# Four layer-norm joints of a two-layer decoder: a split accumulator, a sum read in place, and one centring moved to ScalarE and GpSimd

## The chip, the core and the metric

The kernel runs on one core of a Trainium2 chip. The metric is the device time of one execution in microseconds (us), lower is better. The program is a static list of instructions for each engine: TensorE (PE; its weight loads are listed as PEld), VectorE (DVE), ScalarE (ACT), GpSimd (POOL) and SyncE (SP), which issues most of the DMAs. Each engine works through its own list in order and waits on semaphores for the others.

## The reference

Two layers over 256 positions of 1024 features, all float32. Layer 0 mixes with latent attention, layer 1 with a three-branch sparse attention. Behind each mixer comes a PEER feed-forward block, and after every sub-layer a post-norm, so there are four layer norms:

```python
h = layer_norm(ALPHA * h + mix, ln_g[layer, 0], ln_b[layer, 0])
ffn = peer_ffn(h, p_w_q[layer], p_subkeys[layer], p_u[layer], p_v[layer])
h = layer_norm(ALPHA * h + ffn, ln_g[layer, 1], ln_b[layer, 1])

def layer_norm(x, g, b):
    mu = jnp.mean(xf, axis=-1, keepdims=True)
    var = jnp.mean(jnp.square(xf - mu), axis=-1, keepdims=True)
    return ((xf - mu) * lax.rsqrt(var + LN_EPS) * g + b)
```

The PEER block scores 16384 experts for each token by two sets of 128 sub-keys, keeps 16 for each of 8 heads, and returns the sum of the rows of `p_v` for these experts, weighted by gate times gelu of the dot product with the rows of `p_u`.

## The kernel before

The 256 tokens are two tiles of 128 (`tt` 0 and 1). The kernel computes a PEER block densely: a u phase of 128 steps forms the activations of all experts for most tokens (plain float32 matmuls of 160 columns), and a v phase of 128 steps (`j`) multiplies the gated activations with the rows of `p_v`. The last 64 tokens are done by gathered rows instead (GpSimd's indirect DMAs and VectorE's multiply-accumulate into `gacc`).

**The v phase.** Each step takes a block of `p_v` of 128 rows and 1024 columns. It is split into a high and a low half in the matmul's rounded float32 format (`hi` by ScalarE, line 179; `lo` by VectorE, line 193), and so are the activations (`W`). `v_mm` then issues the matmuls: for token tile 0 three products (high x high, high x low, low x high), for tile 1 two, each over two blocks of 512 columns. Tile 1 holds only 64 tokens that are computed densely; its stationary operand `W[:, P:2P]` carries their high part in one half of its columns and their low part in the other, so its accumulator has the high part's result in partitions 0 to 63 and the low part's in 64 to 127, and the two are added at the end. The accumulators `accs[tt][f]` are four PSUM banks (`pacc`), and four more banks (`mm`, handed out by `self.ps()` in turn) serve everything else.

The last ten steps keep their operands (`keep`), and do tile 0 only. Then tile 0's layer norm runs on VectorE while TensorE catches up with tile 1: the last three steps first, then for the column blocks `f` = 0 and 1 in turn the other seven.

**The joint.** I call the stretch around a layer norm a joint. There are four: two behind the mixers (`out_close`), one behind each PEER block. Behind a PEER block, `sum_1(f)` adds tile 1's block to the residual `hN`: ScalarE copies partitions 64 to 127 of the accumulator to a spare bank (line 988), VectorE adds ALPHA times the residual and the first half (989), then the copy (990), and `ln_stats` takes the statistics of 512 columns (347). `ln_mid` (all four joints) aggregates them (356), takes the square root on ScalarE (357), centres and multiplies the first half by the gain (351), and works out the reciprocal root in short steps of one column (360 to 363). `ln_scale` scales and shifts each half (369); for the second half it first centres (351 again). Where a layer follows (`want_T`), `ln_T` transposes each half on TensorE (line 300), ScalarE casts it into `hT` (383) and VectorE takes the low part (384), and `early_mm` starts the next block's matmuls in between. In the last joint the halves are stored instead (line 371). `lo_aside` has GpSimd do one subtraction of the next block's weights (line 193 on POOL) in the three joints that have a successor.

The order on every engine is that of the code; there is no scheduler.

## Time and profile before

| | |
|---|---|
| median of 3 runs | 1603.38 us (1600.02 to 1606.42) |
| profiled execution | 1603.88 us, span 1601.9 us |
| TensorE busy | 1557.4 us, 97% of the span, 10018 matmuls |
| VectorE busy | 1396.6 us, 87% |
| ScalarE, GpSimd busy | 683.6 us (43%), 536.3 us (33%) |
| matmuls of 512 columns on `hi` and `W` | 1452, line 273 |

A row of the timeline gives the start and the duration in us, the engine, the line of the kernel, the operation, the tile written and the tiles read, the shape, and a count where like instructions are merged; in brackets stands how long the engine had been idle and whom it waited for. Durations of matmuls are modelled and overlap; the distance between their starts is what they cost. A row of a view by windows gives for each engine the busy time and, in brackets, the number of instructions, then TensorE's granted clock (1.00 is full), the DMA engines' share and GB/s.

### The profile page before, as it was taken

How to read it: one execution, taken by the hardware profiler on the slowest of the kernel's cores; microseconds unless marked ns; L12 is line 12 of the kernel's file. 1: busy time of each engine (PE TensorE's matmuls, PEld its weight loads, DVE VectorE, ACT ScalarE, POOL GpSimd, SP SyncE). 2: the span in 40 equal slices, each digit the busy share in tenths (PEclk: the TensorE clock that was granted, in tenths of full speed). 3: DMA queues.
4: the chain of work that ended last, by engine and by line, in shares of the span. 5: the costliest groups of instructions: out<-in, count | busy, mean ns of one | idle time of the engine just before them, and what ended most of it. 6: DMA issues, size and time to landing. Idle time of an engine off the chain costs nothing.

```text
span 1601.9 us, 27548 instructions
## 1 busy us (share of the span) xinstructions
PE 1557.4 (97%) x10018; PEld 1396.3 (87%) x10018; DVE 1396.6 (87%) x3245; ACT 683.6 (43%) x1355; POOL 536.3 (33%) x442
## 2 busy tenths in 40 slices
PE   8999999999999999999997999999999999999997
PEld 6879999999998888888785689999999988888886
DVE  5778898999959999999768779799999959999998
ACT  6555201121225555556456753111221245555553
POOL 2010134434326434340442210234443337543420
PEclk9999999999999999999999999999999999999999
DMA  7627899999999999997573257999999999999992
GB/s 242 198 91 229 347 409 408 408 408 351 389 386 363 370 363 345 360 359 286 187 246 101 79 178 248 403 409 408 409 407 345 375 371 397 377 358 344 359 355 91
DMA packets 140519, 510.76 MB, mean 319 GB/s; under 512 B 14144, under 2 KB 17248, under 8 KB 139296
## 3 DMA queue, kind: packets, MB, share of 16 engines
q1 hardware_dynamic: 90416, 325.75, 55.1%
q0 software_dynamic: 49968, 183.26, 30.1%
q8 instruction: 79, 1.29, 0.3%
q14 instruction: 56, 0.46, 0.1%
HBM read 503.19 MB, written 5.24 MB: 317 GB/s over the span
## 4 chain that ended last, share of the span: by engine, by line
PE 78%; DVE 10%; DMA 8%; ACT 2%; issue 1%; POOL 0%; SPq 0%; ACTq 0%; DVEq 0%; POOLq 0%
PE acc L273 45%; PE mm L273 32%; DMA row<-p_ur,xidx 6%; DVE row L578 3%; PE mm L300 1%; DMA nat<-p_u 1%; DMA raw<-a_wv 1%; DVE hot L759 1%; DVE hot L770 1%; DMA xT<-xT 1%; DVE lo L193 0%; DVE idx L641 0%; DVE bnst L347 0%; ACT hi L179 0%; ACT p L1689 0%
## 5 line engine op out<-in xcount | busy, mean ns | idle before, releaser
L273 PE MATMUL acc<-hi,W 128*128 128x512 f32 x1452 | 409.1, 390 | 0.0
L565 POOL DMA_INDIRECT row<-p_v,gidx x128 | 245.1, 1915 | 305.3 <-DVE gacc L602 238.1
L273 PE MATMUL mm<-xF,nat 128*128 128x160 f32 x2304 | 323.0, 300 | 1.9 <-DMA nat<-p_u 1.9
L273 PEld LDWEIGHTS acc<-hi,W 128*128 128x128 f32 x1452 | 272.5, 188 | 57.5
L273 PEld LDWEIGHTS mm<-xF,nat 128*128 128x128 f32 x2304 | 314.6, 190 | 3.1 <-issue 2.5
L273 PE MATMUL acc<-lo,W 128*128 128x512 f32 x968 | 298.8, 390 | 0.0
L193 DVE TENSOR_TENSOR lo<-raw,hi 128x1024 fp32r<-128x1024 f32 (+1 forms) x203 | 247.3, 1225 | 43.7 <-ACT hi L179 37.1
L179 ACT CAST hi<-raw 128x1024 fp32r<-128x1024 f32 (+1 forms) x207 | 215.1, 1045 | 158.8 <-PE acc L273 115.7
L565 POOL DMA_INDIRECT row<-p_ur,gidx x128 | 139.0, 1086 | 280.0 <-DVE row L578 190.1
L273 PEld LDWEIGHTS acc<-lo,W 128*128 128x128 f32 x968 | 181.7, 188 | 38.5
L179 ACT CAST hi<-spare 128x1024 fp32r<-128x1024 f32 x122 | 128.2, 1051 | 109.0 <-PE acc L273 104.3
L602 DVE SCALAR_TENSOR_TENSOR gacc<-row,ggate,gacc 128x1024 f32<-128x1024 f32 x126 | 161.0, 1278 | 0.0
L193 DVE TENSOR_TENSOR lo<-spare,hi 128x1024 fp32r<-128x1024 f32 x122 | 148.8, 1219 | 10.5 <-ACT hi L179 10.5
L578 DVE SCALAR_TENSOR_TENSOR row<-row,gacc 128x1024 f32<-128x1024 f32 x128 | 155.5, 1217 | 0.0
L273 PE MATMUL mm<-xF,more 128*128 128x160 f32 x896 | 125.7, 299 | 0.0
L273 PE MATMUL mm<-xF,raw 128*128 128x160 f32 x896 | 125.5, 300 | 0.0
L273 PEld LDWEIGHTS mm<-xF,more 128*128 128x128 f32 x896 | 122.6, 190 | 0.0
L273 PEld LDWEIGHTS mm<-xF,raw 128*128 128x128 f32 x896 | 122.5, 190 | 0.0
L795 ACT ACTIVATE A<-acc 128x208 f32<-128x208 f32 (+19 forms) x116 | 37.5, 346 | 194.9 <-DVE A L793 168.2
L885 ACT ACTIVATE A<-mm 128x320 f32<-128x320 f32 (+13 forms) x104 | 38.2, 369 | 173.1 <-PE mm L273 171.4
L905 DVE TENSOR_TENSOR W<-A,W 128x128 fp32r<-128x128 f32 (+1 forms) x512 | 107.1, 250 | 0.0
L565 POOL DMA_INDIRECT row<-p_ur,xidx x64 | 65.9, 1030 | 96.2 <-DVE row L578 43.3
(289 smaller groups left out, 2078.7 us busy)
## 6 DMA issues: line engine op xcount, KB each, us to landing
nat<-p_u SPq DMA_DIRECT2D x144, 512.0 KB, 8.6
spare<-p_v SPq DMA_DIRECT2D x64, 1024.0 KB, 8.8
raw<-p_v SPq DMA_DIRECT2D x63, 1024.0 KB, 8.9
raw<-p_u SPq DMA_DIRECT2D x56, 512.0 KB, 14.3
more<-p_u SPq DMA_DIRECT2D x56, 512.0 KB, 16.2
raw<-p_wq SPq DMA_DIRECT2D x32, 512.0 KB, 4.3
raw<-b_wo SPq DMA_DIRECT2D x12, 512.0 KB, 3.6
raw<-a_wo SPq DMA_DIRECT2D x8, 512.0 KB, 4.1
```

The costliest lines, as they stand in the source:

```text
L179: self.nc.scalar.copy(self.his[i], self.raws[i])
L193: e.tensor_tensor(self.los[i], raw, self.his[i].bitcast(F32), op=OP.subtract)
L273: self.nc.tensor.matmul(out, a, b, start=start, stop=stop)
L300: self.nc.tensor.transpose(out, in_, self.ident[:n, :n])
L565: nc.gpsimd.indirect_dma_start(out=t, out_offset=None, in_=table, in_offset=bass.IndirectOffsetOnAxis(ap=at, axis=0))
L578: nc.vector.scalar_tensor_tensor(t, t, 1.0, x, op0=OP.mult, op1=OP.mult, accum_out=d[:, c:c + 1])
L602: nc.vector.scalar_tensor_tensor(gacc, t, ggate[:, c:c + 1], gacc, op0=OP.mult, op1=OP.add)
L759: tt(h[:, 0:2].rearrange("p w g i s -> p (w g) i s"), self.iota4[:, 0, None].to_broadcast([P, 4, P, 2]), selI[:, t0 // 4].rearrange("p w ( ...
L770: tt(o, oj, x[:, :, None, :].to_broadcast(b4), op=OP.mult)
L795: nc.scalar.activation(x[:, m:n, t0:t0 + 4], pv[:, j0 + m:j0 + n], AF.Copy, scale=sc_)
L885: nc.scalar.activation(y[:, :, n:NU], ps[:, :, n:NU], AF.Gelu)
L905: nc.vector.tensor_tensor(WW[j][:, o:o + c.stop - c.start], slot(j)[:, c], WW[j][:, c].bitcast(F32), op=OP.subtract)
```

## The change

1. Tile 1 gets a third accumulator, taken from the four `mm` banks for the whole v phase. Columns 512 to 1023 go as 512 to 767 and 768 to 1023 into two banks. `v_mm` issues three matmuls for each product of tile 1 instead of two. After the v loop the kept steps run in three parts, and `sum_1` runs after each.
2. `sum_1` reads partitions 64 to 127 of the accumulator in place; ScalarE's copy is gone. The statistics are taken in pieces of 256 columns.
3. The second half's centring of tile 1, in all four joints, leaves VectorE: ScalarE negates the mean and adds it to the half, GpSimd multiplies by the gain (`ln_aside`).
4. The very last half is scaled and stored in two pieces of 256 columns.
5. In the first PEER joint the transposes of tile 0's second half stand behind the second part's matmuls, no longer between them.

```diff
+    def ln_aside(self):
+        nc, w = self.nc, self.lnw[1]
+        z, gb, acc = self.ln_half(1, 1)
+        nc.scalar.mul(w[:, 0:1], w[:, 2:3], -1.0)
+        nc.scalar.activation(z, z, AF.Identity, bias=w[:, 0:1])
+        nc.gpsimd.tensor_tensor(z, z, gb[:, 0, :], op=OP.mult)
...
     def ln_mid(self, tt):
...
         self.ln_center(tt, 0)
+        if tt == 1:
+            self.ln_aside()
...
     def ln_scale(self, tt, hf):
-        if hf == 1:
+        if hf == 1 and tt == 0:
             self.ln_center(tt, 1)
-        self.nc.vector.scalar_tensor_tensor(z, z, self.lnw[tt][:, 7:8], gb[:, 1, :], op0=OP.mult, op1=OP.add)
-        if not self.want_T:
-            self.nc.sync.dma_start(self.O[0, tt * P:(tt + 1) * P, hf * 512:(hf + 1) * 512], z)
+        n = 512 if self.want_T or (tt, hf) != (1, 1) else 256
+        for c in range(0, 512, n):
...
+            accs[1].append(self.ps())
+            part = [(0, 512), (512, 768), (768, 1024)]
...
-                        self.mm(accs[tt][f], xx, ww[:, f * 512:(f + 1) * 512], go, end)
+                        c0, c1 = part[f] if tt else (f * 512, f * 512 + 512)
+                        self.mm(accs[tt][f][:, 0:c1 - c0], xx, ww[:, c0:c1], go, end)
...
-                t = self.ps()
-                c, z = accs[1][f], hN[0:P - GT, 1, f * 512:(f + 1) * 512]
-                nc.scalar.copy(t[0:P - GT], c[P - GT:P])
-                nc.vector.scalar_tensor_tensor(z, z, ALPHA, c[0:P - GT], op0=OP.mult, op1=OP.add)
-                nc.vector.tensor_tensor(z, z, t[0:P - GT], op=OP.add)
+                c0, c1 = part[f]
+                c, z = accs[1][f][:, 0:c1 - c0], hN[:, 1, c0:c1]
+                y = z[0:P - GT]
+                nc.vector.scalar_tensor_tensor(y, y, ALPHA, c[0:P - GT], op0=OP.mult, op1=OP.add)
+                nc.vector.tensor_tensor(y, y, c[P - GT:P], op=OP.add)
+                for c in range(0, c1 - c0, 256):
+                    nc.vector.bn_stats(self.lnst[1][:, self.lnn[1], :], z[:, c:c + 256])
...
             for j in range(P - 3, P):
-                v_mm(j, 1, (0, 1))
+                v_mm(j, 1, (0, 1, 2))
             lo0 = []
-            for f in range(2):
+            for f in range(3):
                 for j in range(P - NT, P - 3):
                     v_mm(j, 1, (f,), False, j == P - 4)
-                    if f == 1 and j == P - 7:
+                    if f == 1 and j == P - 4:
                         lo0.append(self.ln_T(0, 1))
```

VectorE in the last joint, tile 1's sums and statistics up to the aggregation (`acc` and `mm` are accumulators, `bnst` the statistics), before:

```order
L989 SCALAR_TENSOR_TENSOR hN<-hN,acc 64x512 [waits Activation_49]
L990 TENSOR_TENSOR hN<-hN,mm 64x512 [waits DVE_49]
L347 BN_STATS bnst<-hN 128x6 [waits DVE_49]
L989 SCALAR_TENSOR_TENSOR hN<-hN,acc 64x512 [waits Activation_49]
L990 TENSOR_TENSOR hN<-hN,mm 64x512 [waits DVE_49]
L347 BN_STATS bnst<-hN 128x6 [waits DVE_49]
L356 BN_AGGR lnw<-bnst 128x2 [waits DVE_49]
```

and now (the line numbers are those of the changed kernel):

```order
L1008 SCALAR_TENSOR_TENSOR hN<-hN,acc 64x512 [waits PE_49]
L1009 TENSOR_TENSOR hN<-hN,acc 64x512 [waits DVE_49]
L1011 BN_STATS bnst<-hN 128x6 [waits DVE_49]
L1011 BN_STATS bnst<-hN 128x6
L1008 SCALAR_TENSOR_TENSOR hN<-hN,acc 64x256 [waits PE_49]
L1009 TENSOR_TENSOR hN<-hN,acc 64x256 [waits DVE_49]
L1011 BN_STATS bnst<-hN 128x6 [waits DVE_49]
L1008 SCALAR_TENSOR_TENSOR hN<-hN,mm 64x256 [waits PE_49]
L1009 TENSOR_TENSOR hN<-hN,mm 64x256 [waits DVE_49]
L1011 BN_STATS bnst<-hN 128x6 [waits DVE_49]
L366 BN_AGGR lnw<-bnst 128x2 [waits DVE_49]
```

Six steps became ten, and each sum waits for TensorE instead of ScalarE's copy. Behind the aggregation, from the short steps to the end of VectorE's list, before:

```order
L361 SCALAR_TENSOR_TENSOR lnw<-lnw 128x1 [waits DVE_49]
L362 TENSOR_SCALAR lnw<-lnw 128x1 [waits DVE_49]
L363 TENSOR_TENSOR lnw<-lnw 128x1 [waits DVE_49]
L369 SCALAR_TENSOR_TENSOR hN<-hN,lnw,gb 128x512 [waits DVE_49]
L351 SCALAR_TENSOR_TENSOR hN<-hN,lnw,gb 128x512
L369 SCALAR_TENSOR_TENSOR hN<-hN,lnw,gb 128x512 [waits DVE_49]
```

and now:

```order
L373 SCALAR_TENSOR_TENSOR lnw<-lnw 128x1 [waits DVE_49]
L374 TENSOR_SCALAR lnw<-lnw 128x1 [waits DVE_49]
L375 TENSOR_TENSOR lnw<-lnw 128x1 [waits DVE_49]
L383 SCALAR_TENSOR_TENSOR hN<-hN,lnw,gb 128x512 [waits DVE_49]
L383 SCALAR_TENSOR_TENSOR hN<-hN,lnw,gb 128x256 [waits Pool_49]
L383 SCALAR_TENSOR_TENSOR hN<-hN,lnw,gb 128x256
```

The second centring (351) is gone, and the second half's scaling is in two pieces and waits for GpSimd. ScalarE in the joint behind the first mixer, from the root of tile 1 on (`hT` is the transposed activation for the next block), before:

```order
L357 ACTIVATE lnw<-lnw,lneps 128x1
L383 CAST hT<-mm 128x4x128 x3
L179 CAST hi<-raw 128x1024 x2
L823 COPY qN<-acc 128x512 x2
L179 CAST hi<-raw 128x1024 x2
```

and now:

```order
L367 ACTIVATE lnw<-lnw,lneps 128x1
L355 ACTIVATE lnw<-lnw 128x1
L356 ACTIVATE hN<-hN,lnw 128x512
L399 CAST hT<-mm 128x4x128 x3
L179 CAST hi<-raw 128x1024 x2
```

Two instructions stand between the root and the first cast. GpSimd in the same joint, before:

```order
L389 COPY aside<-hN 128x1
L193 TENSOR_TENSOR lo<-raw,hi 128x1024
L620 DMA subT<-p_sub 128x256 x4
L571 DMA xrow<-hD 32x1024 x4
L573 DMA gacc<-hD 64x1024 x2
```

and now:

```order
L405 COPY aside<-hN 128x1
L193 TENSOR_TENSOR lo<-raw,hi 128x1024
L357 TENSOR_TENSOR hN<-hN,gb 128x512
L636 DMA subT<-p_sub 128x256 x4
L587 DMA xrow<-hD 32x1024 x4
```

The product by the gain has come in between the subtraction and the four loads of sub-keys.

More of the change, by code (lines that the diff above doesn't have):

```diff
@@ L335, in ln_start @@
         self.lnw = [self.small.tile([P, 8], F32, tag="lnw", name="lnw") for _ in range(2)]
-        self.lnst = [self.small.tile([P, 2, 6], F32, tag="bnst", name="bnst") for _ in range(2)]
+        self.lnst = [self.small.tile([P, 4, 6], F32, tag="bnst", name="bnst") for _ in range(2)]
+        self.lnn = [0, 0]
     def ln_half(self, tt, hf):
@@ L346, in ln_stats @@
     def ln_stats(self, tt, hf):
-        self.nc.vector.bn_stats(self.lnst[tt][:, hf, :], self.ln_half(tt, hf)[0])
+        self.nc.vector.bn_stats(self.lnst[tt][:, self.lnn[tt], :], self.ln_half(tt, hf)[0])
+        self.lnn[tt] += 1
+    def ln_aside(self):
[4 more added lines that the diff above has]
+        nc.gpsimd.tensor_tensor(z, z, gb[:, 0, :], op=OP.mult)
     def ln_center(self, tt, hf):
@@ L355, in ln_mid @@
         nc, w = self.nc, self.lnw[tt]
-        nc.vector.bn_aggr(w[:, 2:4], self.lnst[tt].rearrange("p a b -> p (a b)"))
+        nc.vector.bn_aggr(w[:, 2:4], self.lnst[tt][:, 0:self.lnn[tt]].rearrange("p a b -> p (a b)"))
         nc.scalar.activation(w[:, 4:5], w[:, 3:4], AF.Sqrt, bias=self.lneps)
@@ L366, in ln_scale @@
         z, gb, acc = self.ln_half(tt, hf)
-        if hf == 1:
+        if hf == 1 and tt == 0:
             self.ln_center(tt, 1)
-        self.nc.vector.scalar_tensor_tensor(z, z, self.lnw[tt][:, 7:8], gb[:, 1, :], op0=OP.mult, op1=OP.add)
-        if not self.want_T:
-            self.nc.sync.dma_start(self.O[0, tt * P:(tt + 1) * P, hf * 512:(hf + 1) * 512], z)
+        n = 512 if self.want_T or (tt, hf) != (1, 1) else 256
+        for c in range(0, 512, n):
+            self.nc.vector.scalar_tensor_tensor(z[:, c:c + n], z[:, c:c + n], self.lnw[tt][:, 7:8], gb[:, 1, c:c + n],
+                                                op0=OP.mult, op1=OP.add)
+            if not self.want_T:
+                c0 = hf * 512 + c
+                self.nc.sync.dma_start(self.O[0, tt * P:(tt + 1) * P, c0:c0 + n], z[:, c:c + n])
     def ln_T(self, tt, hf):
@@ L984, in sum_1 @@
             def sum_1(f):
-                t = self.ps()
-                c, z = accs[1][f], hN[0:P - GT, 1, f * 512:(f + 1) * 512]
-                nc.scalar.copy(t[0:P - GT], c[P - GT:P])
-                nc.vector.scalar_tensor_tensor(z, z, ALPHA, c[0:P - GT], op0=OP.mult, op1=OP.add)
-                nc.vector.tensor_tensor(z, z, t[0:P - GT], op=OP.add)
+                c0, c1 = part[f]
[5 more added lines that the diff above has]
+                    nc.vector.bn_stats(self.lnst[1][:, self.lnn[1], :], z[:, c:c + 256])
+                    self.lnn[1] += 1
             for j in range(P):
@@ L1018, in peer @@
                 if j < P - NT:
-                    v_mm(j, 1, (0, 1), j == 0)
+                    v_mm(j, 1, (0, 1, 2), j == 0)
                     kept.pop(j)
@@ L1034, in peer @@
             for j in range(P - 3, P):
-                v_mm(j, 1, (0, 1))
+                v_mm(j, 1, (0, 1, 2))
             lo0 = []
-            for f in range(2):
+            for f in range(3):
                 for j in range(P - NT, P - 3):
                     v_mm(j, 1, (f,), False, j == P - 4)
-                    if f == 1 and j == P - 7:
+                    if f == 1 and j == P - 4:
                         lo0.append(self.ln_T(0, 1))
-                for x in lo0:
-                    x()
+                while lo0:
+                    lo0.pop()()
                 sum_1(f)
@@ L1046, in peer @@
                     self.lo_aside()
-                self.ln_stats(1, f)
                 if f == 0:
```

## The prediction

> **What bounds the kernel now.** I read the page first (span, busy shares, the chain that ended last), then TensorE's busy time over the value phase, then the timeline engine by engine at the four joints that the change touches.
>
> ```profile
> span 1601.9 us, 27548 instructions
> PE 1557.4 (97%) x10018; PEld 1396.3 (87%) x10018; DVE 1396.6 (87%) x3245; ACT 683.6 (43%) x1355; POOL 536.3 (33%) x442
> PE 78%; DVE 10%; DMA 8%; ACT 2%; issue 1%; POOL 0%; SPq 0%; ACTq 0%; DVEq 0%; POOLq 0%
> ...
> 1320.00:1560.00 240.00, 240.00 (x1057) 198.13 (x1056) 229.65 (x379) 136.91 (x212) 113.59 (x58) 1.00 0.98 366
> ```
>
> TensorE is busy for 97% of the span and makes up 78% of the chain. In 240 us of layer 1's value phase (fourth row; PE is the first pair of numbers) it never idles: 1057 matmuls, 227 ns each. So the change can act in two ways: by what a matmul costs in the value phases, where 512 are added, and by what TensorE waits for at the joints, plus the tail behind the last matmul.
>
> **The split matmuls.** Half of tile 1's columns now take two matmuls of 256 columns instead of one of 512: 128 steps, two products, two layers, 512 more instructions with as many weight loads. The price is the distance between starts, so I take rows that lie back to back:
>
> ```profile
> 1569.18 9.69 PE L273 MATMUL acc<-keep,W 128*128 128x512 f32 x42
> 1578.71 0.63 PE L273 MATMUL acc<-hi,W 128*128 128x512 f32 x2
> ...
> 806.21 1.98 PE L273 MATMUL mm<-hT,hi 128*128 128x256 f32 x16
> 808.02 1.07 PE L273 MATMUL mm<-hT,lo 128*128 128x256 f32 x8
> ...
> 291.82 6.57 PE mm L273 x48
> ```
>
> 42 matmuls of 512 columns take 1578.71 - 1569.18 = 9.53 us, 227 ns each. 16 of 256 columns, each with its own weights, take 808.02 - 806.21 = 1.81 us, 113 ns each: half. The same kind of matmul, so I cost the split at 0. The bounds: 113 ns is the lower end. The upper is the projection with 160 columns, 6.57 us for 48 or 137 ns, where fewer columns cost more; at that price 512 x (2 x 137 - 227) = 24 us. That is another number format, so I take the 256-column row, and keep the other end for a rival.
>
> The Trainium skill ("TensorE: Matmul & The Clock Gate", section "Back-to-back issue gap") gives a warm matmul N/2.4 + 2.5 ns. By its fixed 2.5 ns the split would cost an estimated 512 x 2.5 ns = 1.3 us and the sum below would end at 1607.2. The trace does not show a fixed part, since twice 113 ns is no more than 227 ns.
>
> **The last joint.** Behind the final matmul the time is VectorE's:
>
> ```profile
> 1592.19 0.56 ACT L988 COPY mm<-acc 64x512 f32<-64x512 f32 x1 [2.61 <-PE acc L273]
> ...
> 1589.61 0.68 DVE L989 SCALAR_TENSOR_TENSOR hN<-hN,acc 64x512 f32<-64x512 f32 x1
> 1590.32 0.68 DVE L990 TENSOR_TENSOR hN<-hN,mm 64x512 f32<-64x512 f32 x1
> 1592.78 0.68 DVE L989 SCALAR_TENSOR_TENSOR hN<-hN,acc 64x512 f32<-64x512 f32 x1 [1.05 <-ACT mm L988]
> 1594.94 0.21 DVE L356 BATCH_NORM_AGGREGATE lnw<-bnst 128x2 f32<-128x12 f32 x1
> 1595.25 0.74 DVE L351 SCALAR_TENSOR_TENSOR hN<-hN,lnw,gb 128x512 f32<-128x512 f32 x1
> 1595.91 0.15 DVE L360 RECIPROCAL lnw<-lnw 128x1 f32<-128x1 f32 x1
> 1596.10 0.22 DVE L361 SCALAR_TENSOR_TENSOR lnw<-lnw 128x1 f32<-128x1 f32 x1
> 1596.54 0.16 DVE L363 TENSOR_TENSOR lnw<-lnw 128x1 f32<-128x1 f32 x1
> 1596.74 0.75 DVE L369 SCALAR_TENSOR_TENSOR hN<-hN,lnw,gb 128x512 f32<-128x512 f32 x1
> 1598.19 0.75 DVE L369 SCALAR_TENSOR_TENSOR hN<-hN,lnw,gb 128x512 f32<-128x512 f32 x1
> ...
> 101.06 0.42 DVE L290 TENSOR_TENSOR oT<-mm,oT 128x256 fp32r<-128x256 f32 x1 [0.60 <-ACT oT L289]
> ...
> DMA to landing us min/median/max: 2.0/2.0/2.1
> ```
>
> The copy goes (0.56 us, which VectorE waited for at 1592.78), and the sums come in three parts. A 256-column step takes 0.42 us (row 101.06); the next one starts 0.03 us later if it needs the result (as at 1589.61 + 0.71) and 0.08 us before the end if not (as 1595.25 to 1595.91). Part 0: 0.71 + 0.72 + two statistics at 0.34 = 2.11 us, 1589.61 to 1591.72. Part 1: 0.45 + 0.45 + 0.34, to 1592.96. TensorE's columns are the same, so it ends at 1592.2 as before (start of the copy), and part 2 does not wait for it: 3 x 0.45, to 1594.31. The aggregation so starts 0.63 us earlier. In place of the copy, VectorE's own queue is late.
>
> Call that start A. Before, the chain ends at A + 4.00 (1598.19 + 0.75). Now the second centring (0.75 us) is gone from VectorE, and ScalarE and GpSimd must deliver it. What these take, and how they get along, is read at the first joint.
>
> **ScalarE, GpSimd and the port.**
>
> ```profile
> 115.04 0.30 ACT L357 ACTIVATE lnw<-lnw,lneps 128x1 f32<-128x1 f32 x1 [2.12 <-DVE lnw L356]
> 115.24 0.57 ACT L383 CAST hT<-mm 128x512 fp32r<-128x512 f32 x1
> ...
> 112.93 2.37 POOL L193 TENSOR_TENSOR lo<-raw,hi 128x1024 fp32r<-128x1024 f32 x1
> ...
> 46.12 0.74 POOL L1346 TENSOR_TENSOR ropeO<-ropeU,ropeV 128x256 f32<-128x256 f32 x1 [1.40 <-DVE ropeV L1344]
> ...
> 810.50 1.66 POOL L1346 TENSOR_TENSOR ropeO<-ropeU,ropeV 128x256 f32<-128x256 f32 x1 [4.54 <-DVE ropeV L1344]
> ...
> L193 DVE TENSOR_TENSOR lo<-raw,hi x2: 1215/1490/1766, 810.3 to 811.5; 128x1024 fp32r<-128x1024 f32 x2
> ```
>
> ScalarE's root starts at A + 0.24; one of its 128x1 steps holds the queue for 0.20 us (115.04 to 115.24). The new negation starts at A + 0.44, the shift must wait for its result (0.2 to 0.3 us) and takes about the 0.57 us of the cast: done at A + 1.3. GpSimd's product of 512 columns lies between 0.74 us (256) and 2.37 us (1024): linear, 1.28 us. It starts at A + 1.38.
>
> At 810.5 GpSimd and VectorE both read two SBUF operands: GpSimd took 1.66 us for its 0.74, VectorE 1.77 us for its 1.22. One waits until the other is through. So the product falls in between VectorE's line 361 (A + 1.16) and line 363 (A + 1.60), both with two SBUF operands. I expect line 363 to wait until A + 2.66. The first scaling then runs A + 2.86 to 3.61, the two quarters of the second to A + 4.29 (0.34 and 0.42 us). Last joint: 4.29 - 0.63 - 4.00 = -0.34 us. The last output has half the bytes: between 0 and half of its 2.0 us to landing, I take -0.2, since most of a landing can't be transfer. Together **-0.5 us** (bounds -1.6 to +0.1).
>
> **The two mixer joints.** Both run the shared centring code, so they get the three instructions, but not the shorter sums.
>
> ```profile
> 115.86 1.20 PE L273 MATMUL acc<-hi,hT 128*128 128x512 f32 x4 [1.26 <-ACT hT L383]
> 117.50 0.63 PE L300 MATMUL mm<-ident,hN 128*128 128x128 f32 x4
> ...
> 133.72 1.50 PE L273 MATMUL mm<-subT,qT 128*128 128x128 f32 x12
> ...
> 939.28 1.21 PE L273 MATMUL acc<-hi,hT 128*128 128x512 f32 x4 [1.19 <-ACT hT L383]
> ```
>
> TensorE waits at 115.86 for a cast that now stands on ScalarE behind the two new instructions: negation at 115.24, shift at 115.5, cast at 116.05 instead of 115.24. So 115.86 becomes 116.67. Six matmuls of 227 ns follow, to 118.03, where the transposes of tile 1's first half stood at 117.50. These also need the first scaling, which ends at A + 3.61 instead of A + 2.55: they slip to 118.56. The two delays overlap, the later one counts, and from there on TensorE has no gap that would give it back: **+1.05 us** at each of the two joints. Bounds: +0.5, when the port costs nothing and only ScalarE's delay is left; +1.3, if the product takes 1.5 us. The second scaling may start earlier, but TensorE has other work until then, so that brings nothing here. GpSimd's four subT loads, issued right behind its subtraction of 112.93, now stand behind the product and go out some 2 us later, at about 117.5; they are first read at 133.72, which hides it.
>
> **The first layer's joint.**
>
> ```profile
> 768.15 0.68 DVE L989 SCALAR_TENSOR_TENSOR hN<-hN,acc 64x512 f32<-64x512 f32 x1
> ...
> 774.42 0.21 DVE L356 BATCH_NORM_AGGREGATE lnw<-bnst 128x2 f32<-128x12 f32 x1
> ...
> 777.02 0.66 PE L300 MATMUL mm<-ident,hN 128*128 128x128 f32 x4 [1.27 <-DVE hN L369]
> ...
> L273 PE MATMUL acc<-w,fm x64: 379/379/427, 817.7 to 833.9; 128*60 128x256 f32 x64
> ```
>
> The second half's transposes of tile 0 move behind the second part's matmuls, and the subtraction that follows them moves ahead of the second sum on VectorE. From 768.15 it has a queue without gaps: 2.11 us for part 0, two subtractions at 0.71, 1.24 and 1.35 us for parts 1 and 2, which puts the aggregation at 774.27 instead of 774.42. The port costs 1.06 us ahead of the transposes at 777.02, for which TensorE already waits: **+0.9 us** (bounds -0.2 to +1.1). GpSimd's loads of the next mixer go out some 4 us later; the first weights among them are read at 817.7, some 35 us on, which hides it.
>
> **Sum.** 0 + 1.05 + 0.9 + 1.05 - 0.5 = +2.5 us. The profiled execution took 1603.88 us (span 1601.9), 0.5 us over the median of 1603.38, so against the median I forecast **1605.9 us**. A measurement of this kernel tells about 0.5%, 8 us, from no change; this is within it.
>
> **Rivals.**
> - *The port costs nothing* (GpSimd gets through between the short instructions): the mixers +0.5 each, layer 0 -0.2, the last joint A + 3.5 (product done at A + 2.66, then 0.34 and 0.42 us) and the smaller output, -1.4; sum -0.6, 1602.8 us. Against it stand the rows at 810.5.
> - *The clock.* Longer gaps at the joints let TensorE's clock drop:
>
> ```profile
> 775.86:779.27 3.41, 1.57 (x8) 1.21 (x9) 3.06 (x6) 0.59 (x1) 3.41 (x7) 1.00 0.52 191
> 779.27:786.10 6.83, 6.16 (x18) 4.51 (x17) 4.90 (x5) 1.63 (x2) 0.08 (x1) 0.50 0.96 339
> 113.67:117.09 3.42, 2.15 (x12) 1.60 (x11) 3.18 (x10) 0.77 (x2) 3.42 (x5) 1.00 0.23 49
> 117.09:123.91 6.82, 6.82 (x34) 5.21 (x33) 6.18 (x9) 2.13 (x3) 0.30 (x1) 1.00 0.33 129
> ```
>
> After 3.41 us with 1.57 busy the clock was 0.50 for 6.83 us; after 2.15 busy it stayed 1.00. With the 1.05 us more waiting the first joint comes under 1.57. A halved stretch costs 3.4 us; one or two make 1609 to 1613 us. The Trainium skill (same page, "Why this matters for your kernels") warns only of idle gaps over about 3 us. By that rule no joint would drop; the trace disagrees, having dropped after gaps of at most 1.27 us.
> - *The split costs* (slower): 24 us at the 160-column price, 1629 us. It decides from 16 ns per split pair on, 8 us in 512. Against it: 113 ns in the row of the same kind.
> - *Faster by over 8 us*: no wait of that size stands at the joints; only something that the rows do not show.
>
> **Chances.** Forecast 0.50; port free 0.20; clock 0.19; split 0.07; faster 0.04. Of the clock's 0.19 about 0.03 lies over 1611. So slower 0.10, faster 0.04, same 0.86. The range takes in the port's and the clock's cases and the scatter of the runs before (1600.0 to 1606.4): 1599 to 1613 us.
>
> **What would show it.** Starts of 512- and 256-column matmuls in the value phase 227 and 113 ns apart; at the mixer joints TensorE waiting some 2 us for ScalarE's cast and again for the first scaling; line 375 (the old 363) or the first scaling stretched or late next to GpSimd's product; the last aggregation 0.6 us nearer to the last matmul. I am wrong if the split pairs are over 16 ns dearer, or if the product takes far from 1.3 us.

## The result: 1.2% slower, and the profile after

The changed kernel takes 1622.65 us (median of 4, 1620.55 to 1623.0) against 1602.68 us (also 4): ratio 1.0118, 95% interval 1.0101 to 1.0135. Such a ratio with its interval stands behind every time below, always against the kernel before. The forecast was 1605.9 us in a range up to 1613. The profiled execution took 1620.55 us with a span of 1618.4 us.

The page of the changed kernel, its span and busy times (share of the span, instructions):

```profile
span 1618.4 us, 28589 instructions
PE 1568.7 (97%) x10530; PEld 1422.9 (88%) x10530; DVE 1402.0 (87%) x3250; ACT 684.0 (42%) x1359; POOL 530.5 (33%) x446
```

TensorE is busy for the same 97%, of a longer span: most of the surplus is TensorE work that takes longer. Where it lies, a cut of both spans shows, at marks on TensorE (the first or last start of a kind of matmul; all in us; a mixer joint's stretch is from the first to the last of its 16 transposes):

| stretch | before | after | difference |
|---|---|---|---|
| up to the first mixer's joint | 110.93 | 111.03 | +0.10 |
| that joint | 9.34 | 10.35 | +1.01 |
| projections, to the first u matmul | 48.65 | 49.67 | +1.02 |
| u, layer 0 | 310.34 | 309.88 | -0.46 |
| v, layer 0 | 291.98 | 297.65 | +5.67 |
| last v matmul to the end of the first layer's joint | 8.87 | 9.15 | +0.28 |
| second mixer | 154.62 | 155.49 | +0.87 |
| its joint | 8.96 | 9.95 | +0.99 |
| projections | 48.65 | 49.68 | +1.03 |
| u, layer 1 (with the step into v) | 308.33 | 308.93 | +0.60 |
| v, layer 1 | 291.09 | 296.82 | +5.73 |
| last v matmul to the end | 10.17 | 9.81 | -0.36 |

The differences add up to 16.48 us, that of the spans. 11.4 of them lie in the two value phases, which I had put at 0, and 2.1 in projections whose code nobody touched. First the value phase, 200 us of layer 0, grouped by shape (columns: busy time, whose ends are modelled, and mean; only the counts are used here). Before:

```profile
L273 PE MATMUL acc<-hi,W 128*128 128x512 f32 x530 | 149.1, 389 | 0.0
L273 PE MATMUL acc<-lo,W 128*128 128x512 f32 x352 | 108.5, 389 | 0.0
```

After, the same 200 us:

```profile
L273 PE MATMUL acc<-hi,W 128*128 128x512 f32 x431 | 127.4, 393 | 0.0
L273 PE MATMUL acc<-lo,W 128*128 128x512 f32 x260 | 88.4, 394 | 0.0
L273 PE MATMUL mm<-lo,W 128*128 128x256 f32 x86 | 24.4, 284 | 0.0
L273 PE MATMUL mm<-hi,W 128*128 128x256 f32 x86 | 24.3, 282 | 0.0
L273 PE MATMUL acc<-lo,W 128*128 128x256 f32 x86 | 24.2, 281 | 0.0
L273 PE MATMUL acc<-hi,W 128*128 128x256 f32 x86 | 23.9, 278 | 0.0
```

Before, 882 matmuls of 512 columns fill 200 us, 226.8 ns each. After, 691 and 172 pairs do: at 226.8 ns they would fill 195.7 us, so a pair costs 4.3 us / 172 = 25 ns more than the matmul that it replaces. Step by step: a step of the loop, ten matmuls before and twelve now, took 2.267 us and takes 2.320 us, 53 ns for two pairs. The timeline of one step shows it (start, time, engine, line, tiles):

```profile
1401.79 0.28 PE L273 MATMUL mm<-hi,W 128*128 128x256 f32 x1
1401.91 0.51 PE L273 MATMUL acc<-lo,W 128*128 128x512 f32 x2
1402.26 0.28 PE L273 MATMUL mm<-lo,W 128*128 128x256 f32 x1
1402.38 0.40 PE L273 MATMUL acc<-hi,W 128*128 128x512 f32 x1
```

The second 256 columns take 0.12 us and not 0.113 (the exact starts give 119 and 120 ns), and the group that starts at 1401.91 needs 0.35 us for one matmul of 512 and one of 256 (233 and 118 ns). The 512-column matmuls behind a pair start 238, 235, 232 and 231 ns apart until they are back at 227. So about a third of a pair's price lies in the pair, the rest in the long matmuls behind it.

The first mixer's joint, by engine, after (ScalarE, GpSimd, VectorE, TensorE):

```profile
115.34 0.19 ACT L355 ACTIVATE lnw<-lnw 128x1 f32<-128x1 f32 x1
115.56 0.72 ACT L356 ACTIVATE hN<-hN,lnw 128x512 f32<-128x512 f32 x1
116.19 0.57 ACT L399 CAST hT<-mm 128x512 fp32r<-128x512 f32 x1
...
116.36 1.27 POOL L357 TENSOR_TENSOR hN<-hN,gb 128x512 f32<-128x512 f32 x1 [0.96 <-ACT hN L356]
...
116.50 1.15 DVE L375 TENSOR_TENSOR lnw<-lnw 128x1 f32<-128x1 f32 x1
117.69 0.75 DVE L383 SCALAR_TENSOR_TENSOR hN<-hN,lnw,gb 128x512 f32<-128x512 f32 x1
...
116.81 1.20 PE L273 MATMUL acc<-hi,hT 128*128 128x512 f32 x4 [2.10 <-ACT hT L399]
...
118.58 0.63 PE L300 MATMUL mm<-ident,hN 128*128 128x128 f32 x4
```

All as forecast, with the joint's start 0.1 us later than before: the cast that TensorE waits for comes behind the centring (116.19, forecast 116.05), the product takes 1.27 us, VectorE's 128x1 step next to it takes 1.15 us instead of 0.16, and the transposes stand at 118.58 (forecast 118.56). The second mixer's joint repeats it. The last matmuls of the kernel before, and the last joint after:

```profile
1587.68 4.47 PE L273 MATMUL acc<-keep,W 128*128 128x512 f32 x19
```

```profile
1607.05 1.84 PE L273 MATMUL mm<-keep,W 128*128 128x256 f32 x14
...
1610.96 0.26 DVE L366 BATCH_NORM_AGGREGATE lnw<-bnst 128x2 f32<-128x24 f32 x1
...
1612.62 1.20 DVE L375 TENSOR_TENSOR lnw<-lnw 128x1 f32<-128x1 f32 x1
1613.85 1.54 DVE L383 SCALAR_TENSOR_TENSOR hN<-hN,lnw,gb 128x512 f32<-128x512 f32 x3
```

The aggregation starts 2.07 us behind the last matmul's end (2.79 before: 1594.94 against 1587.68 + 4.47), 0.72 us nearer; line 375, beside GpSimd's product, takes 1.20 us instead of 0.16, and 1.04 us are gone again.

### The profile page after: what moved, and what is told of

Its sections match the earlier page's. It is cut to its first block, busy times and chain, and to the rows that moved or that the text cites. A ratio compares the mean times of both kernels' runs of the same rounds, so it can differ in the third digit from the quotient of the medians.

```text
span 1618.4 us, 28589 instructions
## 1 busy us (share of the span) xinstructions
PE 1568.7 (97%) x10530; PEld 1422.9 (88%) x10530; DVE 1402.0 (87%) x3250; ACT 684.0 (42%) x1359; POOL 530.5 (33%) x446
## 4 chain that ended last, share of the span: by engine, by line
PE 76%; DVE 11%; DMA 8%; ACT 2%; issue 2%; POOL 0%; SPq 0%; DVEq 0%; ACTq 0%; POOLq 0%
PE acc L273 40%; PE mm L273 35%; DMA row<-p_ur,xidx 5%; DVE row L594 3%; DMA nat<-p_u 1%; PE mm L300 1%; DVE hot L775 1%; DVE hot L786 1%; DMA xT<-xT 1%; DMA raw<-s_wT 0%; DVE lo L193 0%; DMA bounce<-ropeO 0%; DVE hN L383 0%; DVE bnst L348 0%; ACT hi L179 0%
## 5 line engine op out<-in xcount | busy, mean ns | idle before, releaser
L273 PE MATMUL acc<-hi,W 128*128 128x512 f32 (+1 forms) x1452 | 385.8, 374 | 0.0
L581 POOL DMA_INDIRECT row<-p_v,gidx x128 | 235.2, 1838 | 325.6 <-DVE gacc L618 259.2
L273 PEld LDWEIGHTS acc<-hi,W 128*128 128x128 f32 x1452 | 256.7, 188 | 40.5
L273 PE MATMUL acc<-lo,W 128*128 128x512 f32 x968 | 275.5, 366 | 0.0
L273 PEld LDWEIGHTS acc<-lo,W 128*128 128x128 f32 x968 | 165.3, 188 | 22.7
```

What stands on the lines that cost most here:

```text
L273: self.nc.tensor.matmul(out, a, b, start=start, stop=stop)
L581: nc.gpsimd.indirect_dma_start(out=t, out_offset=None, in_=table, in_offset=bass.IndirectOffsetOnAxis(ap=at, axis=0))
```

## The experiments

The theory: three causes that add up, namely the split matmuls (A), the layout of SBUF (B) and the second centring by ScalarE and GpSimd (C). Its rival: one cause, for instance that all slower matmuls come from the layout. For B: the statistics tile grew from 2 to 4 records, and the compiled program has every later tile (among them `raw`, `hi`, `lo`, `W`) 64 bytes higher, while `hT` stays.

**The shift alone.** The kernel before, with

```diff
-        self.lnst = [self.small.tile([P, 2, 6], F32, tag="bnst", ...
+        self.lnst = [self.small.tile([P, 4, 6], F32, tag="bnst", ...
```

and the aggregation over records 0 and 1.

> The kernel before, with nothing but the two statistics tiles allocated at the changed kernel's size (4 instead of 2 records): every later tile in SBUF then starts 64 bytes higher, among them hi, lo, W, raw and hN, while hT stays. Theory A (the place in SBUF sets how fast TensorE reads): slower than before, by 5 to 16 us, with the 256-column matmuls of the projections near 119 ns apart instead of 113 to 118, though no instruction changes. Theory S (the split matmuls cost by themselves): 1603 us, the same as before.

1607.07 us (12 runs), ratio 1.0024 (1.0014 to 1.0035). The v stages are unchanged, 291.99 and 291.07 us; the projections slow down. Their 256-column groups of 24 (`hi` the weights, `hT` the moving operand), starts in the kernel before:

```profile
151.99 2.13 PE L273 MATMUL mm<-hT,hi 128*128 128x256 f32 x16
...
155.23 2.07 PE L273 MATMUL mm<-hT,hi 128*128 128x256 f32 x16
...
158.41 0.84 PE L273 MATMUL mm<-hT,hi 128*128 128x256 f32 x5
```

and with the shift:

```profile
150.73 2.15 PE L273 MATMUL mm<-hT,hi 128*128 128x256 f32 x16
...
154.03 2.15 PE L273 MATMUL mm<-hT,hi 128*128 128x256 f32 x16
...
157.32 1.91 PE L273 MATMUL mm<-hT,hi 128*128 128x256 f32 x14
```

From one group to the next (24 matmuls of 256 columns and four short ones) 3.24 and 3.18 us become 3.30 and 3.29. So the shift alone costs 4.4 us, and it is not what slows v. Not all of the 4.4 us is this pace. In the changed kernel, too, the groups run at it, and there the two projections are 2.05 us longer together (table above); in the shift's profile they take 50.56 and 50.32 us, because TensorE also waits once in each for ScalarE's copy of `qT` (0.63 and 0.37 us), as it does in some profiles without the shift. Where the rest lies is not shown.

**Where the shift acts.** The kernel before, with 64 bytes ahead of `hT`, so that `hT` moves too:

```diff
+            const.tile([P, 16], F32, name="room")
             self.lneps = const.tile([P, 1], F32, name="lneps")
```

> The kernel before, with 64 bytes more ahead of hT, so that every large tile, hT among them, moves up by 64 bytes. Theory 'the distance between weights and moving operand' (hi against hT, modulo 128 bytes): the distance is that of before, so the 256-column projections run at 113 and 118 ns again, the stretch from the first joint's transposes to the first u matmul is 48.65 us, time 1602.5. Theory 'where hi itself lies' (64 modulo 128 is the bad place for it): 118 to 120 ns, 50 us and 1607, as when hi moved alone.

1603.19 us (12 runs), ratio 1.0003 (0.9989 to 1.0016). The distances are back at 3.18 and 3.24:

```profile
149.37 2.07 PE L273 MATMUL mm<-hT,hi 128*128 128x256 f32 x16
...
152.55 2.13 PE L273 MATMUL mm<-hT,hi 128*128 128x256 f32 x16
...
155.79 2.07 PE L273 MATMUL mm<-hT,hi 128*128 128x256 f32 x16
```

`hi` lies where it lay with the shift alone; so it is not its place that counts, but its distance to `hT`: by the compiled program's addresses 64 modulo 128 bytes before and here, 0 with the shift alone and in the changed kernel.

**The changed kernel without the shift**, by a filler that makes it 256 bytes:

```diff
+            self.small.tile([P, 48], F32, tag="room", name="room", bufs=1)
             self.raw4 = pool(name="sraw", ...
```

> The changed kernel with a pad of 192 bytes behind the small tiles, so that the later tiles lie 256 bytes higher than before instead of 64: the same place within every 256 bytes. All else is the change. Theory A: back to 1603 to 1607 us (the joints' own terms stay). Theory S: 1620 to 1623 us as the changed kernel.

1622.12 us (5 runs), 1.0113 (1.0095 to 1.0131). The projections are back (48.57 and 48.59 us), and v keeps its 297.66 and 296.81 us. The total hardly falls: 0.5 us by the medians, where the intervals leave about 4 either way. The 4.4 us of the layout are so shown for the kernel before alone. In this profile both mixers' joints ran at half clock (11.44 and 11.09 us), in the changed kernel's neither; whether that holds for the other runs is not shown.

**The changed kernel without the split** (shift and centring kept):

```diff
-            accs[1].append(self.ps())
-            part = [(0, 512), (512, 768), (768, 1024)]
+            part = [(0, 512), (512, 1024)]
...
-                    v_mm(j, 1, (0, 1, 2), j == 0)
+                    v_mm(j, 1, (0, 1), j == 0)
...
-            for f in range(3):
+            for f in range(2):
```

> The changed kernel with tile 1 in two accumulators of 512 columns again (no third bank, two parts at the end); the 64 bytes of shift, the sums in place and ln_aside stay. Theory S: the 11 us that the two value phases grew go away, 1608 to 1611 us. Theory A: some of them stay, since the places do: 1610 to 1622 us.

1612.95 us (6 runs), 1.0054 (1.0038 to 1.0071); v 291.52 and 291.07 us. With the split gone, the 11.4 us of the v stages go: A is shown.

**The realigned kernel with its own centring** by VectorE:

```diff
-            self.ln_aside()
+            pass
...
-        if hf == 1 and tt == 0:
+        if hf == 1:
```

> The changed kernel with the pad of 192 bytes and with the second centring back on VectorE (no ln_aside): against the padded kernel of the same call it shows what ScalarE's and GpSimd's part costs. Both theories: 2 to 4 us less than the padded kernel, by the prediction's terms of 1.05 us at each mixer joint, 0.9 us in layer 0 and about 0.5 us at the end.

1614.59 us (6 runs), 1.0075 (1.0058 to 1.0092); v 297.67 and 296.82 us, the mixer joints 9.35 and 8.97 us, the tail 9.36 us (9.80 with the centring aside: there the wait beside GpSimd's product costs more than the centring brings). The realigned kernel with the centring aside takes 7.5 us more (2 to 4 were expected). This is the base of the next three, which ask why a pair is dear.

**No two short matmuls in a row:** a step's matmuls issued in turn,

```diff
+                one = [(0, f, a == 0, xx, ww) for a, (xx, ww) in enumerate(((xh, hi), (xh, lo), (xl, hi))) for f in (0, 1)]
+                two = [(1, f, a == 0, xx, ww) for a, (xx, ww) in enumerate(((xm, hi), (xm, lo))) for f in (0, 1, 2)]
+                for pair in zip(one, two):
...
-                v_mm(j, 0, (0, 1), j == 0, j == P - 1)
                 if j < P - NT:
-                    v_mm(j, 1, (0, 1, 2), j == 0)
+                    zip_mm(j, j == 0)
```

> As the realigned kernel with its own second centring (1614.6 us; v stages 297.67 and 296.82 us), but the matmuls of a v step are issued in turn, one of token tile 0 (512 columns), one of tile 1, so that no two 256-column matmuls follow each other. Theory 'late loads' (a 256-column matmul is too short to cover the next weight load; two in a row make the loads late, and the 512-column ones behind them, 238, 235, 232, 231 ns instead of 227, pay for catching up): a pair costs about 118 + 120 - 227 = 11 ns instead of 26.7, v stages near 294.9 and 293.9 us, time near 1609. Theory 'each extra matmul costs the same wherever it stands' (53.3 ns a step of two pairs): v stages stay at 297.7 and 296.8, time 1614.6. Theory 'apart is free' (a 512 beside each 256 covers everything): 292.0 and 291.1, time 1603.

1614.83 us (5 runs), 1.008 (1.0066 to 1.0094); v 298.79 and 297.91 us, a little longer than with the pairs together (2.330 us a step instead of 2.320). "Late loads" in the form that blames the neighbourhood falls: apart, an extra matmul is no cheaper.

**The halves in one accumulator:** `accs[1] = [accs[1][0], accs[1][1][:, 0:256], accs[1][1][:, 256:512]]`, summed after the last matmul.

> The same kernel with the two 256-column pieces as two halves of one 512-column accumulator, as before the change, instead of two accumulators; the order of the matmuls is the changed kernel's, and both halves are summed after the last matmul (a few tenths of a us at each end of v). Theory 'the second accumulator' (switching banks, or the bank taken from the transposes' pool, is what costs): v stages back to 292.0 and 291.1 us, time 1603. Theories of the matmul's length ('late loads', 'each extra matmul'): v stages 297.7 and 296.8, time 1614.6 to 1615.5.

1615.31 us (5 runs), 1.009 (1.0074 to 1.0105); v 297.68 and 296.80 us. The third accumulator costs nothing.

**384 + 128 columns:** `part = [(0, 512), (512, 896), (896, 1024)]`.

> The same kernel with the last 512 columns cut as 384 + 128 instead of 256 + 256: the same count of matmuls and of accumulators, another size. Theory 'each extra matmul costs the same': v stages 297.7 and 296.8 us, 1614.6. Theory 'a weight load has a floor' (a matmul starts no sooner than about 113 to 120 ns after the one before it, however few its columns): the 128-column piece takes 113 to 136 ns (136 is the start-to-start of the 128 x 128 matmuls of the u stage) where 57 would be its share of 227, so a pair costs 56 to 80 ns more than 227 and with the catching up behind it up to 110; 256 pairs a layer: v stages 306 to 320 us, time 1632 to 1660.

1642.9 us (5 runs), 1.025 (1.0236 to 1.0264); v 311.47 and 310.56 us. Layer 0's 200 us, by shape (the groups of `lo` are alike: 246, 82 and 82):

```profile
L273 PE MATMUL acc<-hi,W 128*128 128x512 f32 x413 | 126.9, 405 | 0.0
...
L273 PE MATMUL acc<-hi,W 128*128 128x384 f32 x83 | 27.9, 336 | 0.0
...
L273 PE MATMUL mm<-hi,W 128*128 128x128 f32 x82 | 18.4, 225 | 0.0
```

659 of 512 columns and 164.5 pairs in 200 us: 80 ns a pair above 226.8. The 128-column matmul is followed after 60 ns, but the 512-column one behind it takes 286 ns: 346 together, near 227 + 113. I read this as a floor of about 113 ns for a matmul with its own weights, which a shorter one passes on to the next: 57 above the 57 that 128 columns would need, and the rest of the 80, 23 ns, is about the price of every extra matmul (25). That it is the load of the weights which sets the floor fits, but no run shows it. The Trainium skill ("TensorE: Matmul & The Clock Gate", section "LDWEIGHTS (loading the stationary operand)") gives 1/1.2 ns for each column of a weight load, an estimated 107 ns for 128; the floor measured is near it.

**The centring aside alone**, in the kernel before, in the three joints with transposes:

```diff
+        if tt == 1 and self.want_T:
+            self.ln_aside()
...
-        if hf == 1:
+        if hf == 1 and (tt == 0 or not self.want_T):
             self.ln_center(tt, 1)
```

> The kernel before, with nothing but the second centring of tile 1 by ScalarE and GpSimd in the three joints that end in transposes (the last joint is left as before). The prediction's steps alone: first layer's two mixer and expert joints +1.0 us each, 10.35 against 9.34, 13.2 against 12.2 (undisturbed), 9.95 against 8.96: 1605.4 us with the mean clock of before (0.993). Theory 'and the clock': with 2.1 us instead of 1.27 us without a matmul the 3.4 us windows after the joints are run at half clock in some executions, which costs 1.1 us more a joint; mean clock near 0.992, 1606 to 1608.5.

1610.25 us (8 runs), 1.0049 (1.0031 to 1.0067): 7.4 us, by the interval 5 to 11, where the joints' own length makes 3. The first mixer's joint is 11.47 us long here. The granted clock in its windows (columns: us, then busy time and count of PE, PEld, DVE, ACT and POOL, granted clock, DMA share, GB/s):

```profile
113.80:117.21 3.41, 1.31 (x9) 0.90 (x8) 3.20 (x9) 1.58 (x4) 2.44 (x2) 1.00 0.25 84
117.21:120.62 3.41, 3.41 (x12) 2.72 (x11) 2.91 (x6) 0.59 (x1) 2.36 (x5) 0.50 0.65 207
```

and, for TensorE alone, at the same kernel's expert joint and in the changed kernel's first joint:

```profile
779.40:782.80 3.40, 1.67 (x8) 1.00 0.40 110
782.80:786.20 3.40, 2.73 (x9) 0.50 0.38 119
```

```profile
112.00:115.41 3.41, 2.67 (x13) 1.00 0.00 0
115.41:118.82 3.41, 1.90 (x8) 1.00 0.53 154
118.82:122.23 3.41, 3.41 (x20) 1.00 0.52 154
```

The clock is set in windows of 3.41 us, which start elsewhere against the program in each execution. Here a window with 1.31, 1.57 (in the prediction) or 1.67 us of TensorE work is followed by one at 0.50, and one with 1.90 is not. The border is near half a window but not sharp: over all profiles such falls stand behind windows with up to 2.33 us, and one with 1.50 in this kernel's second mixer joint was followed by 1.00. At the mixer's joint a wait of 1.27 us leaves 2.1 us of work in any window, one of 2.10 us may leave 1.31. In the profiles the first mixer's joint ran at half clock in five of the six kernels with ScalarE's centring and no filling, and in none of the ten without it. It costs 1.1 us where it does (11.44 to 11.48 against 10.35).

**The waits filled:** the same, with 14 transposes of the identity ahead of each of the three waits, whose result nobody reads:

```diff
             los.append(self.ln_T(0, 1))
+            self.fill(14)
...
+            if early and hf == 0 and len(los) == 0:
+                self.fill(14)
             los.append(self.ln_T(1, hf))
```

> The same with 14 transposes of the identity, whose result nobody reads, in each of the three waits that the second centring lengthened (about 1.5 us of TensorE work in a wait of 2.1 us). Theory 'the clock': no half-clock window at the joints any more, joints of 10.35, 13.2 and 9.95 us, clock back to 0.993 or above, 1604.5 to 1605.5 us, 1 to 3 us less than without the filling. Theory 'the centring alone costs': the same time as without the filling. If the filling holds up the work behind it, joints longer than 10.4 us at full clock and a time above the unfilled one.

1611.64 us (7 runs), 1.0052 (1.0033 to 1.0071). The joint is 10.32 us long with the clock up:

```profile
112.70:116.11 3.41, 3.05 (x22) 1.00 0.23 18
116.11:119.52 3.41, 3.08 (x14) 1.00 0.62 213
```

but the time is not less. The theory had forecast a mean granted clock of 0.993; it stayed at 0.991 in these runs, as without the filling, so the filling clears the joint and does not raise the clock of the whole. What the clock can explain, the runs themselves tell: of those with a mean clock of 0.990 to 0.992, seven of the centring aside alone take 1610.0 us in the mean and fourteen of the kernel before 1603.9. So 6 us of the surplus stay at equal clock.

**The filling without the centring,** that is, the same two calls of `fill` in the kernel before:

> The kernel before, with the 14 transposes of the identity in the same three waits (1.27 us each without the second centring aside), and nothing else. If the filling is free and the clock is what matters, the time is that of before or 0.5 to 1.5 us less (the window at the expert joint, 6.8 us at half clock in the profile of before, is gone). If the filling itself holds up the work behind it (about 0.3 to 0.7 us a joint, since 14 transposes take about 1.5 us and the waits 1.27 us), 1603.5 to 1605; then the filled centring's 1611.6 less this cost is the time that the centring has at full clock.

1602.24 us (11 runs), 0.9997 (0.9986 to 1.0008). The filling costs nothing and brings nothing. Its profile and that of the filled centring above differ by the centring alone, and they show a cost that the joints' length does not hold. GpSimd issues its own loads for the second mixer (`c_w`), SyncE the mixer's weights (`s_wT`), ScalarE casts them. Without the centring aside, then with it:

```profile
777.43 1.09 POOL L1416 DMA_DIRECT2D w<-c_w  x2
...
781.78 2.61 SPq L125 DMA_DIRECT2D raw<-s_wT  x3
...
787.02 1.05 ACT L179 CAST hi<-raw 128x1024 fp32r<-128x1024 f32 x1 [4.33 <-DMA raw<-s_wT]
```

```profile
785.02 1.09 POOL L1426 DMA_DIRECT2D w<-c_w  x2
...
785.66 2.61 SPq L125 DMA_DIRECT2D raw<-s_wT  x3
...
794.53 1.04 ACT L179 CAST hi<-raw 128x1024 fp32r<-128x1024 f32 x1 [7.93 <-DMA raw<-s_wT]
...
795.62 2.71 PE L273 MATMUL mm<-hT,hi 128*128 128x256 f32 x11 [2.78 <-ACT hi L179]
```

Behind its product, GpSimd issues `c_w` 0.6 us ahead of the weights instead of 4.4, and the cast starts 8.9 us after the weights' issue instead of 5.2: TensorE waits 2.78 us. In the five profiles with the product in the first layer's joint the cast starts 7.0 to 8.9 us after the issue, and TensorE waits 0.8 to 2.8 us for it in four of them; in the fifth, half-clock windows had held TensorE up by as much. In the twelve others it is 3.6 to 6.0 us, and there is no wait. No run moved the loads by themselves.

**The product by VectorE:** VectorE multiplies by gamma just ahead of the last scaling.

```diff
-        nc.gpsimd.tensor_tensor(z, z, gb[:, 0, :], op=OP.mult)
...
+        elif hf == 1:
+            self.nc.vector.tensor_tensor(z, z, gb[:, 0, :], op=OP.mult)
```

> The second centring aside in the three joints, but the product with gamma by VectorE, just ahead of the last scaling, where its centring stood before; ScalarE still subtracts the mean. Theory 'ScalarE' (its pass of 512 columns stands ahead of the cast of hT that TensorE waits for): mixer joints 10.2 to 10.35 us as with GpSimd, time 1608 to 1610. Theory 'GpSimd's hold of the port' (VectorE's small operations and first scaling wait for it): joints back to 9.34 and 8.96 us, 1603 to 1604.

1604.39 us (11 runs), 1.0013 (1.0004 to 1.0022). VectorE's 128x1 step at the first joint, with GpSimd's product and without:

```profile
L373 DVE TENSOR_TENSOR lnw<-lnw 128x1 f32<-128x1 f32 x1 | 1.1, 1149 | 0.0
```

```profile
L372 DVE TENSOR_TENSOR lnw<-lnw 128x1 f32<-128x1 f32 x1 | 0.2, 160 | 0.0
```

ScalarE's part alone costs 1.8 us by the medians, so 5.6 of the 7.4 us come with GpSimd's product. Neither theory had it so. "ScalarE" had the time too long; "GpSimd's hold of the port" had the time nearly right, but not the joints: they did not shrink to 9.34 and 8.96. Both mixer joints fell to half clock in this profile (11.46 and 11.07 us), so their length at full clock is not shown; the first layer's joint is as undisturbed, 12.35 us between its transposes.

**The mixers' joints alone:** the kernel before with `ln_aside`; `self.mixer` is false during tile 1's part of the expert layer's joint.

```diff
+        self.own = not (self.want_T and self.mixer)
+        if tt == 1 and not self.own:
+            self.ln_aside()
...
-        if hf == 1:
+        if hf == 1 and (tt == 0 or self.own):
             self.ln_center(tt, 1)
```

> The second centring aside by ScalarE and GpSimd in the two mixers' joints alone; the first expert layer's joint and the last are as before. If the cost is spread over the three joints: two thirds of 7.4 us, 1607.8. If it is the joints' length alone, 2.0 us: 1604.9. If most of it arises at the expert layer's joint, where the half-clock windows lie in most profiles: 1604.5 to 1605.5 with the mixer joints 10.35 and 9.95 us long.

1607.65 us (7 runs), 1.0027 (1.0014 to 1.0039): two thirds of the 7.4 by the medians, but the interval, 2 to 6 us, hardly tells an even spread from the joints' length alone. In this profile both mixer joints ran at half clock, 4.4 us longer together than before, and TensorE did not wait for the second mixer's weights.

**What is left of the change.** Realigned and unsplit, low half read in place, last output in halves: with the centring aside in the last joint only (`if tt == 1 and not self.want_T`), and without it anywhere.

> What is left of the change when the parts that cost are taken out: realigned, two 512-column accumulators, low half read in place, statistics in 256-column records, the second centring by ScalarE and GpSimd only in the last joint (where no transposes follow), the last output in halves. v stages 292.0 and 291.1 us, projections at 113 and 118 ns as before, the joints with transposes as before or a little shorter (the ScalarE copy of the low half is gone), the tail after the last v matmul 9.6 to 10.0 us (10.17 before, 9.81 changed). By the sum of these 1602.3 us, so the same as before within what can be told; if the joints' cost were not the second centring but the statistics in four records, 1604 to 1606.

> All of the change that has not been shown to cost: realigned, two 512-column accumulators, each half of the second centring by VectorE as before, low half read in place, last output in halves. v stages 291.5 and 291.1 us, joints with transposes as before (9.34, 8.96 us in the mixers). The tail after the last v matmul was 10.10 us unsplit with the aside centring, and 9.36 against 9.80 us in the split kernels without and with it; so 9.6 to 9.7 us here if the aside centring costs the last joint 0.44 us, 10.1 if it does not. Time 1602.2 us, the same as before; 1604 to 1605 if reading the low half in place or the four statistics records cost the joints something.

1605.08 us (11 runs), 1.0014 (1.0004 to 1.0025), and 1604.28 us (12 runs), 1.0006 (0.9993 to 1.002). The tails are 10.03 and 9.67 us: as expected, the last joint is shorter without the centring aside, by 0.36 us, and 0.5 us shorter than before the change. No version beats the kernel before by what can be measured.

## Why the prediction was wrong, point by point

- **The split matmuls, priced at 0: the step that failed.** I took 113 ns from one group of 16 and called it the lower end and the value, because it is half of 227. Other groups of the same shape stood in the same trace at 117 to 120 ns over their 24 matmuls, the slow first one included (the one that starts at 151.99 above, for one: 3.24 us instead of 3.18), which would have made 7 to 13 ns a pair; the rest, matmuls of 512 columns slowed behind it, no row of before showed. Measured: 25 to 27 ns a pair in the steps of the loop, 11.4 us or 22 ns over all 512. The rival "The split costs" had the mechanism, at a price of 47 ns that was too high; its chance was 0.07. Its point of decision, 16 ns a pair, was crossed. The fixed 2.5 ns of the Trainium skill ("TensorE: Matmul & The Clock Gate", "Back-to-back issue gap") would have made an estimated 1.3 us: the trace has about nine times as much.
- **A term that was missing: the layout.** The added records move the other tiles by 64 bytes. That costs 4.4 us alone, of which 2.05 us are the slower pace of the projections; in the changed kernel taking it out won 0.5 us. The sum had no term for it, and nothing in the profile of before could have priced it; the changed addresses could be read in the compiled program.
- **The mixer joints, +1.05 each: right.** +1.01 and +0.99, for the reasons given (late cast, VectorE's step held up beside GpSimd's product, transposes at 118.58). That the profile shows it so clean is luck: of the six kernels with ScalarE's centring and no filling it is the one whose first joint ran at full clock.
- **The first layer's joint, +0.9: right in kind.** The table's +0.28 compares with a joint that ran at half clock in the profile of before. Against the undisturbed 8.47 us of the kernel with everything shifted it is +0.7, and against the 8.11 us of the realigned kernel with its own centring +1.0.
- **The last joint, -0.5: right, -0.36.** The sums brought 0.72 us for 0.63 forecast; the wait beside the product took 1.04 us, where 1.06 was forecast. The 0.2 us for the smaller output did not come: from VectorE's end to the span's end it is 3.0 us before and after.
- **"Which hides it": the second step that failed.** Of GpSimd's loads for the second mixer, some 4 us late, I asked only when they are read themselves. They are under way together with the mixer's first weights, which then come too late for ScalarE's cast: 0.8 to 2.8 us of waiting in four of the five profiles with the product in this joint, 1.64 us in the changed kernel's own. The second mixer's stretch is 155.8 us long in the mean of these five (154.5 to 157.9) and 153.7 in the twelve others (151.9 to 155.2); of this difference of 2.1 us 1.8 are there behind the wait, 13 us into the stretch.
- **The price of the centring aside in the whole, mis-sized.** It costs 7.4 us alone (5 to 11), where the joints' steps make 3.0. The late loads add about 2, and the lower granted clock of these runs 1 to 2. What is left, about 1 us, is within the scatter. This sum is read from profiles and clocks; no run shows it by itself. A half-clock window adds 1.1 us to the first mixer's joint (in five of six profiles), not 3.4 us as the rival "The clock" had it.
- **The clock by gaps.** The Trainium skill (same page, "Why this matters for your kernels") warns of gaps over about 3 us; here a window fell to half clock behind a wait of 2.10 us. The trace decides: here the fall goes with the work in a window, not with the length of one gap.

By themselves the three causes make 11.4 + 4.4 + 7.4 = 23.2 us, less what the shorter sums save: 0.4 us at the expert joint (8.11 in the realigned kernel with its own centring, against 8.47) and 0.4 at the end (9.81 against 10.17, with its own centring aside). That is 22.4, for 20.0 measured. Taken out of the changed kernel, the split won 9.7 us, the shift 0.5, and the centring 7.5 where the shift was out already: 17.7; with all three out the time is 1604.28. The intervals of the three allow either difference; the split and the centring are large both ways, the layout only in the first.

## What to carry to other kernels

Cutting a matmul in two costs as many starts and weight loads as it adds, here 25 ns a piece, in every repetition of the loop; what it saves is paid once, at the joint. Price a shape by all its groups in the trace, not by the group that fits, and ask where the spread comes from; what the long matmuls behind a short one pay shows only in a stream that mixes them. When an engine that issues loads is made to wait, ask not only when these loads are read, but what else they will be under way with. When a small tile grows, compare the addresses of the large ones before and after, and put them back with a filler.

## What the runs showed of the hardware that I had not expected

- The distance in SBUF between a matmul's weights and its moving operand changes its pace: 256-column matmuls with 64 bytes modulo 128 between them run at 113 to 114 or 116 to 118 ns behind the first of a group, whole groups in one state or the other; with 0, at 118 to 120 ns. Moving both together changes nothing.
- In these streams an extra matmul is no cheaper behind a long one than behind a short one (2.330 us a step against 2.320), and costs the same with an accumulator of its own or without (v 297.67 and 297.68 us).
- A matmul of 128 columns may start its successor after 60 ns; the successor then takes 286 ns instead of 227.
- The clock's windows: 3.41 us, free of the program, half clock after some windows with about half of them busy or less (1.31, 1.57, 1.67 and 2.00 us fell, one with 1.50 and one with 1.90 did not). That, and no change in the work, is 1.1 us at the first joint.
- With another queue's loads issued 0.6 instead of 4.4 us ahead of it, a load of weights was ready for its cast after 8.9 instead of 5.2 us.
- An operation of 128x1 elements stretched from 0.16 to 1.15 us beside a GpSimd product of two SBUF operands.
